# Local attention in two-step tiles beside RWKV's recurrence, with one PSUM bank for both chains

## The chip, the cores and the metric

One core of a Trainium2 chip runs the whole kernel. The metric is the device time of the program in microseconds; the median of three runs counts. A profiled execution of the same program gives the trace. Engines: PE is TensorE's matmul, PEld its weight load, DVE VectorE, ACT ScalarE, POOL GpSimd, SP SyncE, which here only issues DMAs.

## What is computed

Two layers over 512 latent and 256 context tokens, 1024 columns. Each layer: a modulated norm; one input projection whose columns go to four mixers (HGRN2, RWKV-7, windowed attention with sinks, multi-head latent attention); one output projection; a feed-forward block (dense in layer 0, eight experts in layer 1). Two of the mixers matter here.

```python
def rwkv7_scan(r, w, k, v, kk, b, s0, reverse):      # once forward, once backward
    def step(S, inp):
        r_t, w_t, k_t, v_t, kk_t, b_t = inp
        sa = jnp.einsum('bhvk,bhk->bhv', S, kk_t)
        S = S * w_t[:, :, None, :] - sa[..., None] * b_t[:, :, None, :] + v_t[..., None] * k_t[:, :, None, :]
        return S, jnp.einsum('bhvk,bhk->bhv', S, r_t)
...
def swa_mixer(p_lat, p_ctx, sink, cos, sin, ctx_out):
    ...
    mask = (jnp.abs(W + i - j) <= W)[None] & (s_abs >= 0) & (s_abs < T)
    s_loc = jnp.einsum('bkgnqd,bknsd->bkgnqs', qb, kw).astype(F32) * scale
    s_ctx = jnp.einsum('bkgnqd,bkcd->bkgnqc', qb, kc).astype(F32) * scale
    logits = jnp.concatenate([jnp.where(mask, s_loc, -jnp.inf), s_ctx, sink_l], axis=-1)
    prob = jax.nn.softmax(logits, axis=-1)
    o = (jnp.einsum('bkgnqs,bknsd->bkgnqd', prob[..., :3 * W], vw)
         + jnp.einsum('bkgnqc,bkcd->bkgnqd', prob[..., 3 * W:3 * W + Lc], vc))
    ...
```

Latent attention (`mla`) is softmax attention of four heads, in which a latent query sees all 768 keys and a context query the 256 context keys. In layer 1 (`last`) only latent tokens have an output.

## The kernel before

The program is written with a tile framework: the Python code issues instructions in an order, tiles of one name rotate through `bufs` buffers, and the framework sets the waits; the trace shows that it also moves an instruction that is ready ahead of one that is not. Generators are woven by `weave` (L243): each has a rate, and in every round the generators with rate 1 do one step, up to their next `yield`.

`mixers` (L1310) runs, per layer: projections with HGRN2's recurrence woven in (`columns`, L1415), then **the recurrence stage** (L1469 to 1480), then **the attention stage** (L1497 to 1529), then the rest of the output projection.

In the recurrence stage two directions (`rw_dir`, L648) each walk 12 chunks of 64 tokens in six pairs. For each pair a preparation (`rw_pair`, L718) loads decay W and key kk from DRAM (`s.rd`), forms the products BK and AR (r times W on POOL, L753), the matrices G, and an inverse by doubling: five levels of three steps. It has 19 steps; at most two preparations of a direction live at a time. Its matmuls go to four banks (`a00` to `a11`). A chain (`rw_chain`, L831) then does four steps a chunk: R, U, Z (the new state) and O (the output), each a group of matmuls into a bank of its direction (`c0` or `c1`, `psc`, L838) and an eviction; R and U are copied by VectorE and ScalarE, one half each (`pad`, L628). A third generator, `attention_prep` (L1449, rate 0.5), loads and prepares the queries and keys of both attentions in two banks named `hg` (`hps`, L347), and layer 0 computes two groups of modulation (`ada`, L414) through the same banks. Eight banks in all.

In the attention stage five generators are woven at rate 1: the read-outs of RWKV and HGRN2, `mla` (L1229), `swa` (L1164) and the loads of the first output weights. `swa` does, per block of 128 queries and per g, two tiles (kv = 0, 1): scores against two context key blocks and up to three neighbours, band additions in PSUM (L1186), `softmax` (L1107: sink copy, maximum, exponential with its sum, reciprocal, scaling, transposes into `pt`, copies into `PT`), then `heads_pv` (L1137: probabilities times values, two per key block and tile). Both attentions share three two-bank score buffers `sc`, one bank `pt` and one bank `pv`. `emit` (L1487) splits a result into two parts (a ScalarE cast and a POOL subtraction) for the output projection.

A matmul of float32 data is recorded as two instructions, a transpose as one.

## Time and profile before

| | us |
|---|---|
| median of 3 runs | 2664.5 (2660.79 to 2669.68) |
| profiled execution | 2658.14 |
| its span in the trace | 2656.0 |
| recurrence stage, layer 0 / layer 1 | 380 to 587 / 1669 to 1858 |
| attention stage, layer 0 / layer 1 | 587 to 731 / 1858 to 1958 |

A stretch is given in microseconds from the span's start. Busy times of an engine are the union of its instructions; PE's ends are modelled, and its matmuls overlap, so counts and distances between starts say more than its share. A line number can be that of a helper: L638 is `flip`, L328 `turn`, L633 `pad`, L276 the subtraction of a split.

### The profile page before, as it was taken

To read this page: it belongs to the slowest core of one execution; us is meant where nothing else is said; L and a number is where in the kernel's file an instruction comes from. 1 tells how busy PE (TensorE), PEld (TensorE's weight loads), DVE (VectorE), ACT (ScalarE), POOL (GpSimd) and SP (SyncE) were. 2 spreads that over 40 slices of the span, in tenths; PEclk is the share of its full clock that TensorE was granted. 3 is DMA by queue.
4 is the path that set the end of the run, shared out by engine and by line. 5 is a ranking of instruction groups with operands and counts; after the bars stand their busy time and mean duration, and the time that the engine had idled before them with its cause. 6 is when DMAs were issued, how large, how long until landed. Compare 5 with 4: busy or idle time off the path is not lost. (4 is left out here: it accounts for less than half of the span.)

```text
span 2656.0 us, 46639 instructions
## 1 busy us (share of the span) xinstructions
PE 2411.9 (91%) x18131; PEld 1991.5 (75%) x18131; DVE 1649.4 (62%) x3055; ACT 1240.9 (47%) x2348; POOL 487.5 (18%) x665
## 2 busy tenths in 40 slices
PE   7998779989998999999999998788996999999994
PEld 3887556666587888888877876566674898898993
DVE  5567946557568644344337597665745667667765
ACT  4744426556723211211237454565653556555653
POOL 1012345531011000000020222763202000000002
PEclk9999879999998999999999999799998899999997
DMA  6222142111053533334322323210213888887885
GB/s 225 84 82 93 65 139 69 32 39 56 1 165 125 153 117 115 120 114 128 112 71 67 97 73 120 72 30 8 72 36 101 271 266 274 277 268 259 264 273 175
DMA packets 190311, 339.28 MB, mean 128 GB/s; under 512 B 26465, under 2 KB 111201, under 8 KB 190081
## 3 DMA queue, kind: packets, MB, share of 16 engines
q1 hardware_dynamic: 183024, 310.39, 36.8%
q0 software_dynamic: 6480, 23.73, 2.5%
q8 instruction: 145, 2.38, 0.4%
q10 hardware_dynamic: 576, 2.10, 0.2%
q14 instruction: 86, 0.70, 0.1%
HBM read 305.88 MB, written 28.84 MB: 126 GB/s over the span
## 5 line engine op out<-in xcount | busy, mean ns | idle before, releaser
L288 PE MATMUL big<-hhi,hiw 128*128 128x512 f32 (+1 forms) x1504 | 523.7, 349 | 9.7 <-ACT hhi L510 3.8
L289 PE MATMUL big<-hlo,hiw 128*128 128x512 f32 (+1 forms) x1504 | 521.9, 347 | 1.7 <-DVE hlo L511 1.7
L290 PE MATMUL big<-hhi,low 128*128 128x512 f32 (+1 forms) x1504 | 519.7, 346 | 3.5 <-DVE low L276 2.3
L275 ACT CAST hiw<-raww 128x512 fp32r<-128x512 f32 (+3 forms) x208 | 158.3, 766 | 563.2 <-PE big L289 362.2
L288 PEld LDWEIGHTS big<-hhi,hiw 128*128 128x128 f32 x1504 | 286.3, 191 | 56.4 <-ACT hhi L510 8.1
L290 PEld LDWEIGHTS big<-hhi,low 128*128 128x128 f32 x1504 | 285.3, 190 | 44.4 <-DVE low L276 3.9
L289 PEld LDWEIGHTS big<-hlo,hiw 128*128 128x128 f32 x1504 | 285.9, 190 | 42.3 <-issue 4.0
L276 DVE TENSOR_TENSOR lom<-rawm,him 128x1024 fp32r<-128x1024 f32 x176 | 215.1, 1224 | 126.7 <-ACT him L275 125.1
L276 DVE TENSOR_TENSOR low<-raww,hiw 128x512 fp32r<-128x512 f32 (+3 forms) x202 | 184.7, 920 | 124.9 <-ACT hiw L275 123.3
L275 ACT CAST him<-rawm 128x1024 fp32r<-128x1024 f32 x176 | 184.3, 1047 | 148.8 <-PE sml L289 65.7
L288 PE MATMUL sml<-xh,him 128*128 128x256 f32 x528 | 151.9, 288 | 0.0
L289 PE MATMUL sml<-xl,him 128*128 128x256 f32 x528 | 149.4, 283 | 0.0
L290 PE MATMUL sml<-xh,lom 128*128 128x256 f32 x528 | 149.4, 283 | 0.0
L276 DVE TENSOR_TENSOR lov<-rawv,hiv 128x1024 fp32r<-128x1024 f32 x88 | 107.5, 1222 | 39.8 <-ACT hiv L275 39.6
L288 PE MATMUL sml<-him,xh 128*128 128x256 f32 x440 | 127.3, 289 | 0.6 <-DVE xl L276 0.6
L289 PE MATMUL sml<-lom,xh 128*128 128x256 f32 x440 | 125.3, 285 | 0.0
L290 PE MATMUL sml<-him,xl 128*128 128x256 f32 x440 | 125.1, 284 | 0.0
L289 PE MATMUL big<-gl,hiw 128*128 128x512 f32 (+1 forms) x352 | 119.5, 339 | 0.0
L288 PE MATMUL big<-gh,hiw 128*128 128x512 f32 (+1 forms) x352 | 118.9, 338 | 0.0
L290 PE MATMUL big<-gh,low 128*128 128x512 f32 (+1 forms) x352 | 118.2, 336 | 0.0
L275 ACT CAST hiv<-rawv 128x1024 fp32r<-128x1024 f32 x88 | 92.4, 1050 | 53.3 <-PE y L290 43.1
L455 DVE SCALAR_TENSOR_TENSOR raww<-raww,cb 128x1024 f32<-128x1024 f32 x56 | 68.6, 1225 | 69.1 <-DMA raww<-in_wadt 67.9
(551 smaller groups left out, 5618.3 us busy)
## 6 DMA issues: line engine op xcount, KB each, us to landing
rawm<-in_m SPq DMA_DIRECT2D x176, 512.0 KB, 5.1
rawv<-in_m SPq DMA_DIRECT2D x88, 512.0 KB, 4.9
raww<-in_wadt SPq DMA_DIRECT2D x56, 512.0 KB, 3.6
raww<-in_w SPq DMA_DIRECT2D x52, 512.0 KB, 3.9
raww<-in_winc SPq DMA_DIRECT2D x92, 256.0 KB, 2.9
raww<-in_wout SPq DMA_DIRECT2D x16, 512.0 KB, 3.7
wadt<-in_wadt SPq DMA_DIRECT2D x16, 512.0 KB, 4.2
raww<-in_w SPq DMA_DIRECT2D x16, 448.0 KB, 3.3
```

Source lines behind the costliest of these rows:

```text
L275: s.S.copy(hi, src)
L276: (eng or s.V).tensor_sub(lo, src, hi)
L288: s.E.matmul(out, ah, bh, start=start, stop=False)
L289: s.E.matmul(out, ah, bl, start=False, stop=False)
L290: s.E.matmul(out, al, bh, start=False, stop=stop)
L455: V.scalar_tensor_tensor(x, w, 1.0, cb[v], op0=OP.mult, op1=OP.mult, accum_out=m[:, v:v + 1])
```

## The change

Local attention moves from the attention stage into the recurrence stage: `attention_prep` goes on into `swa`, and its rate is 0.85 in layer 0 and 0.65 in layer 1. `softmax` is cut in three: maximum, exponential, and turn (reciprocal, scaling, transposes, copies). `swa` now has two steps a tile: the scores of a tile, then the turn of the tile before; then maximum and exponential of the new tile. The probabilities go to two fixed tiles (`turns`) in place of three rotating ones, and the exponentials to two buffers of 641 columns, which also serve as scratch for the ropes.

In PSUM, both chains take their R, U and Z from one bank `c`; O goes to the bank `pt`, which local attention uses for its transposes and its outputs; the two `hg` banks are replaced by one two-bank score buffer `sc`, of which `hps` takes the first half. Four `a` banks, `c`, `pt` and `sc` are eight. In SBUF, r leaves the pool that lives through the recurrence: its columns are written to DRAM behind the RWKV projection, and each preparation that needs r loads its part (`rq`). In the attention stage a generator `windows` splits local attention's results, 256 tokens a step, and `mla` keeps its buffers.

```diff
--- before.py
+++ after.py
@@ -346,6 +346,8 @@
 
     def hps(s):
 
+        if not s.nhg:
+            return s.ps("sc", 1024)[:, :512]
         return s.pp.tile([128, 512], F32, name="hg", bufs=s.nhg)
 
     def seg_gemm(s, lhsT, rhs, ntok, use, tag=None):
@@ -738,8 +740,10 @@
         P.tensor_copy(We, W[:, :, :, e:e + 1])
         AR = z['AR']
         BK = tp.tile([128, 2, 2, 2, 64], F32, name="BK" + nm)
-        kv, rv = tp.tile([128, 2, 2, 64], F32, name="kkq", bufs=2), v(g['r'])
+        kv, rv = (tp.tile([128, 2, 2, 64], F32, name=n, bufs=2) for n in ("kkq", "rq"))
         s.Q.dma_start(kv, v(s.rd[:, :2]))
+        if want:
+            s.Q.dma_start(rv, v(s.rd[:, 6:8]))
         bk = BK.rearrange("p c q t n -> p q t c n")
         V.tensor_mul(bk[:, 0], Wi, v(g['b']))
         P.tensor_mul(bk[:, 1], Wi, v(g['k']))
@@ -835,8 +839,8 @@
         AR, RP, UP = z['AR'], z['RP'], z['UP']
         c, vq, nm = ch - lo, z['v'], f"{d}"
 
-        def psc():
-            return s.ps("c" + nm)[:, :128].rearrange("p (t n) -> p t n", t=2)
+        def psc(tag="c"):
+            return s.ps(tag)[:, :128].rearrange("p (t n) -> p t n", t=2)
 
         def plus_state(out, a):
             for p in range(2):
@@ -861,7 +865,7 @@
             V.tensor_mul(Zn, Zn, We[:, :, c].to_broadcast([128, 2, 64]))
             yield
         if not (last and lo >= 8):
-            pO = psc()
+            pO = psc("pt")
             s.flip(pO, lambda p: G[:, c, 1, p, 1], lambda p: vq[:, c, p], True, False)
             s.flip(pO, lambda p: G[:, c, 0, p, 1], lambda p: UP[:, p], False, False)
             plus_state(pO, 1)
@@ -1104,9 +1108,9 @@
         for h, o in out or ():
             s.V.tensor_add(o[h, :LAT], x[h, :LAT], t[h])
 
-    def softmax(s, w, ps, scale, extra, tp, eng):
-
-        E, V, S = s.E, s.V, s.S
+    def softmax_max(s, w, ps, scale, extra, tp):
+
+        V = s.V
         n = w
         if extra is not None:
             V.tensor_copy(ps[:, w:w + 1], extra)
@@ -1117,15 +1121,21 @@
             V.tensor_scalar_mul(nm, nm, -scale)
         else:
             V.tensor_scalar(nm, nm, scale, -1.0, op0=OP.mult, op1=OP.mult)
-        pe = tp.tile([128, T], F32, name="pe", bufs=3)
+        return nm, n
+
+    def softmax_exp(s, ps, nm, n, scale, tp, pe):
         sm = tp.tile([128, 1], F32, name="sm", bufs=4)
-        S.activation(pe[:, :n], ps[:, :n], AF.Exp, bias=nm, scale=scale, accum_out=sm)
+        s.S.activation(pe[:, :n], ps[:, :n], AF.Exp, bias=nm, scale=scale, accum_out=sm)
+        return sm
+
+    def softmax_turn(s, w, pe, sm, p, eng):
+
+        E, V, S = s.E, s.V, s.S
         V.reciprocal(sm, sm)
         if eng is S:
             S.activation(pe[:, :w], pe[:, :w], AF.Copy, scale=sm)
         else:
             eng.tensor_scalar_mul(pe[:, :w], pe[:, :w], sm)
-        p = tp.tile([128, 6, 128], F32, name="PT", bufs=3)
         for a in range(0, w, 512):
             n = min(512, w - a)
             pt = s.ps("pt", 512, 1)
@@ -1134,8 +1144,15 @@
             (S.copy if a == 0 else V.tensor_copy)(p[:, a // 128:(a + n) // 128].rearrange("p a b -> p (a b)"), pt[:, :n])
         return p
 
-    def heads_pv(s, out, PT, nk, vts):
-        pv = s.ps("pv")[:, :128]
+    def softmax(s, w, ps, scale, extra, tp, eng):
+
+        nm, n = s.softmax_max(w, ps, scale, extra, tp)
+        pe = tp.tile([128, T], F32, name="pe", bufs=3)
+        sm = s.softmax_exp(ps, nm, n, scale, tp, pe)
+        return s.softmax_turn(w, pe, sm, tp.tile([128, 6, 128], F32, name="PT", bufs=3), eng)
+
+    def heads_pv(s, out, PT, nk, vts, tag="pv"):
+        pv = s.ps(tag)[:, :128]
         for j in range(nk):
             for i in range(2):
                 s.E.matmul(pv[64 * i:64 * i + 64], vts(i, j), PT[i][:, j], start=j == 0, stop=j == nk - 1)
@@ -1161,38 +1178,53 @@
                     S.copy(qp[g][hv[h], h, LAT:], q[hv[h], g, LAT:])
             yield
 
-    def swa(s, l, last, q, k, qp, vt, band, tp, emit):
-        E, V, S, P = s.E, s.V, s.S, s.P
-        nq = LAT if last else T
-        sk = s.sk
+    def swa(s, l, last, q, k, qp, vt, band, tp, turns):
+
+        E, V, S = s.E, s.V, s.S
+        sk, scale = s.sk, HD ** -0.5
+
+        def keys_of(blk):
+            return [4, 5] + ([n for n in (blk - 1, blk, blk + 1) if 0 <= n < 4] if blk < 4 else [])
+
+        def scores(blk, g, kv):
+            keys = keys_of(blk)
+            ps = s.ps("sc", 1024)
+            runs, at = [(512, 256)], 0
+            if blk < 4:
+                b0, nb = keys[2], len(keys) - 2
+                runs += [(128 * b0, 256)] + ([(128 * b0 + 256, 128)] if nb == 3 else [])
+            for ko, kn in runs:
+                E.matmul(ps[:, at:at + kn], qp[g][:, kv, 128 * blk:128 * blk + 128], k[:, ko:ko + kn], start=True, stop=True)
+                at += kn
+            for j, kb in enumerate(keys):
+                if j >= 2 and kb != blk:
+                    m = band[:, 0 if kb < blk else 1]
+                    V.tensor_add(ps[:, 128 * j:128 * j + 128], ps[:, 128 * j:128 * j + 128], m)
+            return ps
+
+        def turned(blk, g, kv, pe, sm):
+            keys = keys_of(blk)
+            PT.append(s.softmax_turn(128 * len(keys), pe, sm, turns[kv], (V, S)[kv]))
+            if kv:
+                s.heads_pv(q[:, g, 128 * blk:128 * blk + 128], PT, len(keys), lambda i, j: vt[:, keys[j], i], "pt")
+                PT.clear()
+        PT, ahead = [], None
         for blk in range(4 if last else 6):
             for g in range(2):
-                qs = slice(128 * blk, 128 * blk + 128)
-                keys = [4, 5] + ([n for n in (blk - 1, blk, blk + 1) if 0 <= n < 4] if blk < 4 else [])
-                w = 128 * len(keys)
-                PT = []
                 for kv in range(2):
-                    ps = s.ps("sc", 1024, 3)
-                    runs, at = [(512, 256)], 0
-                    if blk < 4:
-                        b0, nb = keys[2], len(keys) - 2
-                        runs += [(128 * b0, 256)] + ([(128 * b0 + 256, 128)] if nb == 3 else [])
-                    for ko, kn in runs:
-                        E.matmul(ps[:, at:at + kn], qp[g][:, kv, qs], k[:, ko:ko + kn], start=True, stop=True)
-                        at += kn
-                    for j, kb in enumerate(keys):
-                        if j >= 2 and kb != blk:
-                            m = band[:, 0 if kb < blk else 1]
-                            V.tensor_add(ps[:, 128 * j:128 * j + 128], ps[:, 128 * j:128 * j + 128], m)
+                    ps = scores(blk, g, kv)
+                    if ahead:
+                        turned(*ahead)
+                    yield
                     h = 2 * kv + g
-                    PT.append(s.softmax(w, ps, HD ** -0.5, sk[:, h:h + 1], tp, (V, S)[kv]))
-                s.heads_pv(q[:, g, qs], PT, len(keys), lambda i, j: vt[:, keys[j], i])
-                if blk % 2:
-                    c = slice(128 * blk - 128, 128 * blk + 128)
-                    emit(4 + g, c, q[:, g, c])
-                yield
+                    nm, n = s.softmax_max(128 * len(keys_of(blk)), ps, scale, sk[:, h:h + 1], tp)
+                    pe = tp.tile([128, 641], F32, name="pe", bufs=2)
+                    ahead = blk, g, kv, pe, s.softmax_exp(ps, nm, n, scale, tp, pe)
+                    yield
+        turned(*ahead)
+        yield
         for t in range(2):
-            s.tap(f"sw{l}{t}", q[:, t, :nq], slice(0, nq))
+            s.tap(f"sw{l}{t}", q[:, t, :LAT if last else T], slice(0, LAT if last else T))
 
 
     def mla_prep(s, l, last, cq, ckv, psf, scr):
@@ -1325,7 +1357,7 @@
             with ExitStack() as rx:
                 rp = rx.enter_context(s.pool("rec", side="right"))
                 g = {}
-                for n in ('r', 'k', 'b'):
+                for n in 'kb':
                     g[n] = rp.tile([128, 2, T], F32, name="rw" + n)
                 hgt, rwt = (x.rearrange("p a (c n) -> p (a c n)", n=64).rearrange(tok, c=12, t=2) for x in (hgo, rwo))
                 with ExitStack() as ax:
@@ -1336,7 +1368,7 @@
                     s.hhi = hh.tile([128, KT, T], F32R, name="hhi")
                     s.hlo = hh.tile([128, KT, T], F32R, name="hlo")
                     g['c0'] = s.wp.tile([128, 9], F32, name="rwc0")
-                    g['v'] = s.wp.tile([128, 2, T], F32, name="rwv")
+                    g['r'], g['v'] = (s.wp.tile([128, 2, T], F32, name=f"rw{n}") for n in 'rv')
                     g['yg'] = s.wp.tile([128, T], F32, name="rwyg")
                     g['tmp'] = lambda: s.wp.tile([128, T], F32, name="rwtmp", bufs=2)
                     g['yw'], g['ya'] = rwo[:, 0], rwo[:, 1]
@@ -1415,6 +1447,7 @@
                         def columns():
 
                             yield from s.rw_project(l, last, g)
+                            Q.dma_start(s.rd[:, 6:8, :nq], g['r'][:, :, :nq])
                             yield from s.rw_prep(l, last, g, s.wp)
                             if l == 0:
                                 s.clear_rows()
@@ -1437,7 +1470,7 @@
 
                     if l == 0:
                         yield s.ada(range(4, 6), lambda: tp.tile([128, 2, 512], F32, name="wada"),
-                                    s.hps, lambda: scr[0]), 6 / 64
+                                    s.hps, lambda: tp.tile([128, 2, 512], F32, name="wada")[:, 0]), 6 / 64
 
                 sq, cq, (ckv, sk) = hq, hk[0], (hz[0][:, i] for i in range(2))
                 f = it.rearrange("p a b c d -> p (a b c d)")
@@ -1466,18 +1499,20 @@
                     w = bp.tile([128, 512], F32, name="wk")
                     wk.append(w)
                     Q.dma_start(wk[0], s.I['wukv'][l])
+                    PT = f[:, 768:1408], tp.tile([128, 640], F32, name="PT1")
+                    yield from s.swa(l, last, sq, sk, qp, svt, band, tp, [x.rearrange("p (a b) -> p a b", a=5) for x in PT])
                 with s.pool("b") as tp, s.pool("pb", 1, PSUM) as s.pp:
                     done = set(), set()
-                    s.nhg = 2
+                    s.nhg = 0
                     wq, wk = bp.tile([128, 768], F32, name="wq"), []
-                    scr = [tp.tile([128, 512], F32, name=f"scr{i}") for i in range(2)]
+                    scr = [tp.tile([128, 641], F32, name="pe", bufs=2) for i in range(2)]
                     s.mskf = tp.tile([128, 2, 6, 64], F32, name="mskf")
                     mg = tp.tile([128, 512], F32, name="mg")
                     s.mg = mg.rearrange("p (d q n) -> p d q n", d=2, q=2)
                     Q.dma_start(mg, s.I['cst'][:, C_MG:C_MG + 512])
                     Q.dma_start(s.mskf, s.I['cst'][:, C_MSK:C_MSK + 768].rearrange("p (d h n) -> p d h n", d=2, h=6))
                     s.weave(*((s.rw_dir(d, last, g, rwt, *done, tp), 1) for d in range(2)),
-                            (attention_prep(s.hps), 0.5), *modulation(tp, scr))
+                            (attention_prep(s.hps), (0.85, 0.65)[l]), *modulation(tp, scr))
             with ExitStack() as ox:
                 hh = ox.enter_context(s.pool("oh"))
                 hhi = hh.tile([128, KT, T], F32R, name="hhi")
@@ -1514,10 +1549,15 @@
                         s.ow = ox.enter_context(s.pool("ow"))
                         for m in range(2):
                             load(m)
+                    def windows():
+                        for o in range(0, nq, 256):
+                            for k in range(2):
+                                emit(4 + k, slice(o, o + 256), sq[:, k, o:o + 256])
+                            yield
                     s.weave((s.rw_read(l, last, ld['v'], ld['yg'][:, 0], rwt, dp, emit), 1),
                             (s.hg_read(l, last, ld['gt'], hgt, dp, emit), 1),
                             (s.mla(l, last, cq, ckv, cstm, wq.rearrange("p (a b) -> p a b", a=2), wk[0], tp, dp, emit), 1),
-                            (s.swa(l, last, sq, sk, qp, svt, band, tp, emit), 1), (weights(), 1))
+                            (windows(), 1), (weights(), 1))
 
                     pss += [s.ps("sc", 1024, 3) for m in range(2)]
                     for o in range(0, nq, 256):
@@ -1973,7 +2013,7 @@
         s.yb = dp.tile([nrow, D], F32, name="yb")
         s.gd = dp.tile([128, 12, T], F32, name="gd")
         s.vd = dp.tile([128, 12, 128], F32, name="vd")
-        s.rd = dp.tile([128, 6, T], F32, name="rd")
+        s.rd = dp.tile([128, 8, T], F32, name="rd")
         s.setup()
         with ExitStack() as s.fx:
             s.mixers(0, False, s.I['xT'])
```

## Rows read from the trace of the kernel before

**Rows 1.** The page's first part: busy time, share of the span, instructions per engine.

```profile
PE 2411.9 (91%) x18131; PEld 1991.5 (75%) x18131; DVE 1649.4 (62%) x3055; ACT 1240.9 (47%) x2348; POOL 487.5 (18%) x665
```

**Rows 2.** Busy us per stretch: PE, PEld, DVE, ACT, POOL; clock, DMA share, GB/s.

```profile
380.00:390.00 10.00, 0.26 (x2) 0.26 (x4) 1.26 (x3) 4.30 (x8) 9.41 (x22) 0.50 0.82 213
390.00:587.00 197.00, 179.70 (x2365) 126.83 (x2364) 120.85 (x358) 107.03 (x344) 100.27 (x167) 0.98 0.15 42
587.00:638.00 51.00, 44.77 (x247) 30.39 (x246) 37.76 (x104) 28.68 (x64) 17.32 (x22) 0.97 0.18 57
638.00:731.00 93.00, 86.10 (x587) 55.84 (x587) 57.21 (x170) 69.36 (x161) 7.33 (x10) 1.00 0.09 32
1669.00:1690.00 21.00, 11.14 (x60) 7.96 (x60) 9.95 (x22) 8.92 (x16) 13.88 (x30) 0.50 0.44 119
1690.00:1858.00 168.00, 146.08 (x2128) 110.18 (x2129) 111.22 (x327) 98.43 (x327) 90.05 (x148) 0.99 0.08 20
1858.00:1902.00 44.00, 40.80 (x229) 26.42 (x227) 34.62 (x98) 27.69 (x60) 15.63 (x20) 1.00 0.27 84
1902.00:1958.00 56.00, 55.28 (x386) 37.72 (x384) 38.05 (x97) 42.78 (x88) 2.91 (x4) 1.00 0.06 20
```

**Rows 3.** Waits of the loader, 390 to 587: for whom, total us, times, longest.

```profile
PEld a L638 <- POOL AR L753: 8.8, 7, 1.9
PEld a L638 <- issue: 8.1, 35, 0.8
PEld a L638 <- ACT AP L633: 4.8, 15, 0.8
PEld a L328 <- DVE TU L817: 4.1, 12, 0.8
PEld c L638 <- issue: 3.7, 22, 0.2
```

**Rows 4.** Line L1181 alone, local attention's scores: PE, PEld busy in 1930 to 1958.

```profile
1930.00:1958.00 28.00, 0.00 (x0) 0.00 (x0) 1.00 0.00 1
```

**Rows 5.** Timeline, latent attention alone in layer 1: start us, duration, engine, instruction.

```profile
1940.88 1.52 PE L1141 MATMUL pv<-PT,mvt 128*64 128x128 f32 x22
...
1946.98 1.52 PE L1141 MATMUL pv<-PT,mvt 128*64 128x128 f32 x22
```

**Rows 6.** Waits of PE in layer 0's attention stage, 587 to 731: the largest.

```profile
PE pt L1133 <- ACT PT L1134: 4.3, 11, 0.9
```

**Rows 7.** Groups of 587 to 731 by form: busy us, mean ns; idle before, releaser.

```profile
L1141 PE MATMUL pv<-PT,it 128*64 128x128 f32 x176 | 17.2, 283 | 0.6 <-ACT mvt L1274 0.6
...
L1186 DVE TENSOR_TENSOR sc<-sc,it 128x128 f32<-128x128 f32 x24 | 7.0, 297 | 8.2 <-PE sc L1181 7.8
...
L1115 DVE TENSOR_REDUCE nm<-sc 128x1 f32<-128x641 f32 x8 | 6.6, 822 | 0.2
L1122 ACT ACTIVATE pe<-sc,nm 128x641 f32<-128x641 f32 x8 | 6.4, 796 | 4.6 <-DVE nm L1117 4.5
...
L1134 DVE COPY PT<-pt 128x128 f32<-128x128 f32 x8 | 2.3, 288 | 1.2 <-PE pt L1133 1.2
```

**Rows 8.** Timeline of the stage's end; last, from tile acc, the chains' U matmuls.

```profile
581.12 0.29 DVE L860 TENSOR_TENSOR Z<-c,Z 128x128 f32<-128x128 f32 x1
...
582.79 0.44 PE L638 MATMUL c<-v,G 128*64 128x128 f32 x4 [0.38 <-DVE xm L870]
...
583.92 0.26 ACT L633 COPY acc<-c 64x128 f32<-64x128 f32 x1 [2.50 <-DVE acc L633]
...
585.09 0.26 ACT L633 COPY UP<-c 64x128 f32<-64x128 f32 x1 [0.91 <-DVE UP L633]
...
L638 PE MATMUL c<-acc,TF x96: 270/273/324, 435.7 to 584.4; 128*64 128x128 f32 x96
```

**Rows 9.** Line L742, the kk loads: SP ns min, median, max; landing us.

```profile
L742 SPq DMA_DIRECT2D kkq<-rd x24: 359/365/468, 381.6 to 1788.2; - x24
...
DMA to landing us min/median/max: 2.0/2.2/2.3
```

**Rows 10.** Timeline: a 64-column weight load behind a 128-column transpose, in the recurrence.

```profile
508.67 0.19 PEld L638 LDWEIGHTS c<-acc,TF 128*64 128x64 f32 x2 [0.17 <-issue]
```

## Prediction

> **What bounds the kernel now.** I first read the page's engine totals [rows 1]: TensorE is marked busy 91% of the span, VectorE 62%, ScalarE 47%. That is an average over stages, so next comes the table by stretch [rows 2]. Each layer has a recurrence stage (380 to 587 in layer 0, 1669 to 1858 in layer 1) and behind it an attention stage (587 to 731 and 1858 to 1958) that ends where the output projection's first matmul starts. Only these four stretches, 640 us, are touched, apart from one store in the projections.
>
> The recurrence is not held by one engine. After its start, its weight loader (PEld) is busy 126.83 of 197 us in layer 0 and 110.18 of 168 in layer 1, so 70 and 58 us of it are idle; VectorE is at 61 and 66%, ScalarE at 54 and 59% [rows 2]. The loader's waits are many and short, at most 2 us each, on POOL, ScalarE and VectorE in turn [rows 3]: six small streams (per direction one chain and two preparations) step through all engines.
>
> The attention stage is different. Late in layer 1, when local attention has run out of score matmuls [rows 4] and latent attention runs alone, the order of TensorE repeats itself: from one group of 22 prob-times-value matmuls to the next pass 6.10 us [rows 5], nearly all of it filled. In that time two tiles of six key blocks of 128 are done, so **a key block costs 0.51 us** of a stage that TensorE sets. Its waits confirm it: of 144 us of layer 0's stage, the largest wait of TensorE is 4.3 us in total [rows 6].
>
> **What leaves the attention stage.** Local attention has 24 tiles in layer 0: eight of five key blocks, eight of four, eight of two, 88 blocks; layer 1 has 72 (eight of five, eight of four). The 176 prob-times-value matmuls of layer 0, two per block, agree [rows 7]. At 0.51 us, 88 and 72 blocks are 45 and 37 us, 82 together. The opening of that stage (latent projections, rope, its DMAs, read-outs: 51 us in layer 0, 44 in layer 1, with VectorE at 74 and 79% [rows 2]) had local attention as its filler. Without it some of its dependent steps show; I deduct 2 us per layer: **-78 us**. From below: if the opening kept half its length, 25 and 22 us, and 16 tiles of 3.05 us follow, layer 1 needs 71 us against 100 (-29), and layer 0, with eight small tiles more of two blocks (8 us), 82 against 144 (-62); that is 91 in all. From above, if the opening stays as long as it is, nothing of what ran inside it is won, and about 35 us remain. I keep 78, nearest to the measured period. The splits of the results (windows) stay in this stage beside latent attention: 0.
>
> **What it costs in the recurrence.** If nothing were hidden, 82 us come back; if all fits into the 70 and 58 us of idle loader time, 0. Which is nearer is read from VectorE, since it is the engine nearest to full there. Local attention's VectorE groups in layer 0 are twelve, from the band additions to the last small probability copy [rows 7]; with one division, one maximum, one negation and one sink copy per tile they sum to 43 us, in layer 1 to 33. VectorE would then have 120.85 + 43 = 164 us and 111.22 + 33 = 144 us of work [rows 2]. No stretch of these stages shows it above 79%; the 51 us opening, with as many streams, has 74%. At 74% the stages need 221 and 195 us, against 197 and 168: +24 and +27. At 79% they need 208 and 183: +11 and +15. ScalarE (107 + 44 us in 221, 68%) stays under the 75% that it shows in 638 to 731 [rows 2]. I take 74%: **+51 us**.
>
> **The shared bank.** Both chains now rotate through one bank for the three steps R, U and Z; O goes to the bank of the transposes. With nobody in the way, at the end of the stage, R holds its bank from 582.79 to 584.18 and U from 584.23 to 585.35 [rows 8]; Z, with eight matmuls like U's and one addition of 0.29 us in place of U's two copies, about 1.0 us (an estimate from those). Three uses take 3.5 us, 24 chunks 84 us, and the first U of the stage stands at 435.7 [rows 8], 151 us before its end. So the bank has 67 us to spare over 72 uses, and the chains mostly wait for the preparations anyway. TensorE, though, waits in order: behind a blocked R stand the preparations' matmuls. I count six chunks at the end, where no preparation is left, each with one ScalarE copy of 0.26 us more: 1.5 us per layer, **+3 us**; bounds 0 and, if each of 144 uses in both layers waits for one copy, +37.
>
> **Small parts.** The r columns take a detour through DRAM: one store in the projections, which TensorE bounds and 0, at most 4 (twice what the load below takes). Then 20 loads more on SP's queue, each right behind the kkq load, which lands in 2.2 us and costs SP 0.365 us [rows 9]; behind them on SP stand the second direction's loads, and POOL's product with r waits for them. That product is what TensorE's loader waits for longest in the recurrence, 8.8 us in layer 0 [rows 3], but it also stands behind ScalarE's exponential of W and POOL's own product before it, so the load has a cover: 0; where that is gone, 0.4 us a time over 20 times, 8 us. The preparation of attention runs at 0.85 and 0.65 steps a round in place of 0.5: it moves earlier inside the same stage, 0. Its matmuls, and layer 0's modulation with its four loads a group, borrow the one two-bank score buffer: local attention stands behind them. The 50 steps of layer 0 after some 14 preparing ones need 75 rounds at 0.85, about the rounds of the recurrence (19 steps a preparation, two at a time, three times, plus the start and the last chain); so a lag would show as a tail. I take 0, at most 27 us (eight tiles left over, each with nothing beside it at 3.4 us for maximum, exponential, scores and copies).
>
> **A rule weighed.** In the recurrence a 64-column block that follows a 128-column one shows a gap of 0.17 us marked "issue" [rows 10]; the loader's issue waits sum to some 12 us of layer 0 in its two largest rows [rows 3]. The Trainium skill, TensorEngine Tiling (Array Packing), section Tiling Modes, says that changing the tiling mode drains TensorE. The trace agrees in kind. It speaks against this change, since scores and transposes use the whole array and are now strewn among 64-column blocks. By rows: some three blocks a tile, two changes each at 0.17 us, 40 tiles: 41 us; in the attention stage about a quarter of them was paid already, so +30. As most issue gaps of today hide in waits for other engines, I don't add it; it is a rival.
>
> **Sum.** -78 + 51 + 3 = -24 us. The profiled execution took 2658.1 us, its span 2656.0; it lies 6.4 us under the median 2664.5 of the runs shown. So 2634 on its own scale, **2640** as a median.
>
> **The rivals.** *Hidden well:* VectorE reaches 79% or more and the opening shrinks as TensorE allows: -85 + 26 + 0 = -59, some 2605. For it speaks the idle loader; against it that each piece needs all three engines. *Width changes:* the 30 us are paid in full: -24 + 30 = +6, 2670, no change. A lag of eight tiles gives the same (+27). *Slower by longer steps:* the recurrence's length is a chain of steps, some 75 per layer, 146 in both. Each step evicts through VectorE and ScalarE, in order, and may find a softmax piece of 0.8 us (maximum 822 ns, exponential 796 ns [rows 7]) ahead of it. At 0.53 us more a step the 78 us are used up; at 0.68 us, 99 + 3 - 78 = +24: 2688. For it: the loader waits today on just such evictions; against it: with TensorE full of other work, part of a step's delay is overlapped by the other streams. That the bank alone decides it I hold for unlikely, as its 67 us of room must go first.
>
> **How the numbers follow.** Forecast 2640 (2625 to 2655) with 0.38, hidden well 0.25, width changes or a lag 0.15, longer steps 0.22. A measurement of this kernel can tell about 0.3%, 8 us, from no change. The forecast's upper end gives 0.02 to no change, the longer steps' lower end 0.01. So faster 0.61, same 0.17, slower 0.22. The range reaches from 2600 (0.05 lies below, where even more is hidden) to 2688 (half of the longer steps lies above): 2600 to 2688.
>
> **What would show it.** Right: latent attention's first score matmul some 20 to 30 us after the recurrence ends, then 3.05 us a tile; the attention stages near 100 and 66 us; the recurrence near 231 and 216 us with VectorE at 74%; no long wait on the c bank. Wrong: local attention's matmuls behind the last chain (a lag), issue gaps that double (widths), waits of loads for AP, TU and TT that grow from 0.3 to 0.6 us a time (longer steps), or waits of c matmuls on the other direction's copies (the bank).

## The result and the profile after

The median is 2683.45 us against 2663.08 us for the kernel before in the same runs: ratio 1.0069, 95% interval 1.0049 to 1.009. The change makes the kernel slower by some 20 us; 2640 was forecast. The profiled execution has a span of 2677.6 us, 21.6 more than before.

The engines' totals hardly moved against [rows 1]. First part of the page of the changed kernel:

```profile
PE 2421.7 (90%) x18131; PEld 1995.0 (75%) x18131; DVE 1643.8 (61%) x3055; ACT 1245.4 (47%) x2348; POOL 489.2 (18%) x665
```

From here on a **recurrence** reaches from the first product of AR with BK to latent attention's first q matmul, and an **attention stage** from there to the first matmul of the output projection. By stretch (busy us of PE, PEld, DVE, ACT, POOL; clock, DMA share, GB/s), first the two recurrences of the kernel before at these borders, then both stages of the changed kernel, in which the attention stage is cut at latent attention's first score matmul:

```profile
389.74:586.72 196.98, 179.68 (x2364) 126.81 (x2364) 120.85 (x358) 107.02 (x344) 100.51 (x167) 0.98 0.15 42
1679.49:1857.44 177.95, 153.87 (x2172) 115.16 (x2172) 118.58 (x339) 101.56 (x335) 96.60 (x159) 0.96 0.09 24
```

```profile
387.81:660.58 272.77, 239.24 (x2712) 168.38 (x2712) 157.92 (x494) 146.59 (x440) 100.69 (x167) 0.94 0.13 36
660.58:683.12 22.54, 20.36 (x71) 11.05 (x72) 14.96 (x30) 11.62 (x28) 19.54 (x26) 0.92 0.37 121
683.12:746.78 63.66, 59.87 (x401) 38.77 (x400) 41.92 (x105) 47.77 (x99) 4.81 (x7) 1.00 0.15 49
1697.08:1917.57 220.49, 196.74 (x2468) 146.09 (x2468) 143.39 (x443) 132.75 (x399) 98.43 (x159) 0.96 0.09 24
1917.57:1939.55 21.98, 16.81 (x54) 7.98 (x55) 13.52 (x26) 10.42 (x24) 16.73 (x22) 1.00 0.35 98
1939.55:1983.05 43.50, 42.16 (x263) 27.16 (x262) 29.21 (x64) 32.31 (x59) 1.45 (x2) 1.00 0.18 60
```

The attention stages gave back more than hoped: 86.2 and 65.5 us against 144 and 100 (587 to 731 and 1858 to 1958, [rows 2]), 93 us less. The recurrences took more than that: 272.8 and 220.5 us against 197.0 and 178.0, **118 us more**. VectorE, which was to be their limit at 74%, stands at 58 and 65%. PE is marked busy 88 and 89% of them.

One stretch of layer 0 shows at first sight why. Timeline of the changed kernel: two successive Z additions of the chains, between them the modulation's use of the score buffer sc, local attention's scores (L1197), and an O (bank pt) with the U behind it:

```profile
555.85 0.29 DVE L864 TENSOR_TENSOR Z<-c,Z 128x128 f32<-128x128 f32 x1
...
564.90 0.14 PEld L427 LDWEIGHTS sc<-wada,scp 128*32 128x32 f32 x4 [0.17 <-DMA wada<-in_wada]
...
567.80 1.32 PE L1197 MATMUL sc<-hz,hz 128*128 128x256 f32 x6
...
581.21 0.39 PE L640 MATMUL pt<-UP,G 128*64 128x128 f32 x4
...
582.43 0.27 DVE L635 COPY UP<-c 64x128 f32<-64x128 f32 x1
...
588.91 0.28 DVE L864 TENSOR_TENSOR Z<-c,Z 128x128 f32<-128x128 f32 x1
```

For 33 us no new state Z is made. The modulation holds the score buffer and waits for a DMA; local attention's scores come after it; O waits for pt, which local attention's turns use ahead of it; and the next U cannot be copied to UP, of which a direction has one, until O has read it. It looks like the cause, and it is what I tested first. It turned out to be a small part of it at most: layer 1 grew by 42 us with no such stall, its longest pause between two Z being 16 us (14 before).

### The profile page after: what moved, and what is told of

The parts are those of the page before. It is cut to its first block, busy times and chain, and to the rows that moved or that the text cites. A ratio compares the mean times of both kernels' runs of the same rounds, so it can differ in the third digit from the quotient of the medians.

```text
span 2677.6 us, 46644 instructions
## 1 busy us (share of the span) xinstructions
PE 2421.7 (90%) x18131; PEld 1995.0 (75%) x18131; DVE 1643.8 (61%) x3055; ACT 1245.4 (47%) x2348; POOL 489.2 (18%) x665
## 5 line engine op out<-in xcount | busy, mean ns | idle before, releaser
L276 DVE TENSOR_TENSOR lov<-rawv,hiv 128x1024 fp32r<-128x1024 f32 x88 | 107.5, 1222 | 33.7 <-ACT hiv L275 33.5
L797 POOL TENSOR_TENSOR Gm<-G,mskf 128x256 f32<-128x256 f32 x120 | 93.1, 785 | 149.3 <-PE a L640 146.9
```

Of the source, the lines that this page charges most:

```text
L276: (eng or s.V).tensor_sub(lo, src, hi)
L797: P.tensor_mul(x, G[:, :, 0, :, 0], s.mskf[:, 1 - d, i][:, None, None].to_broadcast(sh))
```

## The experiments

Theory 1: O queues in pt behind local attention. Theory 2: the bank c that both chains share. Theory 3: local attention's own instructions on the engines. Later expectations name finer forms: R is theory 1 again, P is theory 3 by TensorE's time, Q is theory 3 by softmax pieces that lie ahead of the chains' evictions on VectorE and ScalarE. The recurrence of the kernel before, in two later runs that leave it alone, took 198.0 us twice in layer 0 and 177.9 twice in layer 1, so a stage repeats within about 1 us.

**O back in c.**

```diff
-            pO = psc("pt")
+            pO = psc()
```

> The changed kernel with one edit: each chain's O goes back to the bank that its R, U and Z use (c), so that pt serves local attention alone. Theory 1 (my new one): O queues in pt behind the turns of local attention, whose tiles come late, and because each direction has one UP tile, which O reads, the next chunk's U cannot be written until O is done; the chains stand still. Then layer 0's recurrence falls from 281 us to 245 or less, layer 1's from 232 to 205 or less, and the time from 2683 to 2615-2640. Theory 2 (the one bank c for two chains is what costs): c gets a quarter more work, both recurrences grow, 2690 or more. Theory 3 (local attention's own instructions lie ahead of the chains' on the engines): 2675-2690, no stage moves by over 6 us.

Measured: 2700.3 us (ratio 1.0145, 1.0122 to 1.0168); windows of its recurrences:

```profile
389.31:662.11 272.80, 239.25 (x2712) 169.20 (x2712) 159.18 (x494) 146.53 (x440) 101.15 (x167) 0.92 0.13 36
1699.32:1933.00 233.68, 204.74 (x2469) 152.11 (x2469) 144.00 (x443) 133.00 (x399) 99.00 (x159) 0.91 0.09 23
```

The 33 us without a Z are gone (the longest pause in layer 0 is now 21 us), but layer 0's recurrence has the same length to 0.1 us and layer 1's is 13 us longer. The time is the one forecast for theory 2, but its growth shows in layer 1 alone. Theory 1 falls as the main cause. How much the stall was worth this run does not tell, since O in c has a price of its own: 13 us in layer 1, 8 of them as PE's busy time at a granted clock of 0.91 instead of 0.96. In layer 0 the price and what the stall had cost may have cancelled.

**The chains' bank plan alone**, in the kernel before.

```diff
-        def psc():
-            return s.ps("c" + nm)[:, :128]...
+        def psc(tag="c"):
+            return s.ps(tag)[:, :128]...
-            pO = psc()
+            pO = psc("pt")
```

> The kernel before with the bank plan of the chains alone: both directions take R, U and Z from one bank c, O goes to a bank pt of its own that nothing else uses; local attention stays in the attention stage and the two hg banks stay. Theory 1 and theory 3: the shared bank costs little; 2663-2675, recurrences 207-213 and 189-195 us. Theory 2: recurrences of 235 or more and 210 or more, 2700 or more.

Measured: 2676.5 us (1.0054, 1.0032 to 1.0076); the recurrences take 6.7 and 7.5 us more:

```profile
389.33:592.97 203.64, 183.13 (x2365) 128.09 (x2365) 117.52 (x358) 108.13 (x345) 101.55 (x167) 0.97 0.14 41
1689.35:1874.77 185.42, 157.47 (x2173) 117.98 (x2173) 114.83 (x339) 102.45 (x335) 97.65 (x159) 0.94 0.09 23
```

The shared bank costs 14 us by itself: real, but an eighth of the 118.

**The modulation moved to the attention stage** (there at rate 1, with three score buffers), alone and together with O in c.

```diff
-                            (attention_prep(s.hps), (0.85, 0.65)[l]), *modulation(tp, scr))
+                            (attention_prep(s.hps), (0.85, 0.65)[l]))
...
-                            (windows(), 1), (weights(), 1))
+                            (windows(), 1), (weights(), 1), *modulation(tp))
```

> The changed kernel with layer 0's two groups of modulation moved from the recurrence stage to the attention stage, where three score buffers stand; the one score buffer of the recurrence stage is then local attention's and its preparation's alone. Theory 1 with its cause in layer 0 (the modulation holds the score buffer from 398 to 440 and from 547 to 568 us, local attention is late by that, and O waits behind it): layer 0's recurrence falls by 30-50 us to 230-250, its attention stage grows by 5-15, layer 1 is unmoved, time 2640-2665. Theory 2 and theory 3: the recurrence falls by under 10 us, 2675-2690.

> Both edits at once: O back in the bank c and the modulation in the attention stage. Theory 1: what is left of the growth of the recurrences is the work of local attention and the shared c: layer 0 215-235, layer 1 195-205, time 2590-2630; the two edits overlap in layer 0, so their gains do not add there. Theory 2: 2685 or more. Theory 3: 2670-2690.

Measured: 2683.1 us and 2708.8 us. In the first, layer 0's recurrence is 246.0 us (26.8 less) and its attention stage 113.0 (26.8 more):

```profile
389.63:635.63 246.00, 221.07 (x2673) 163.59 (x2673) 155.84 (x486) 144.68 (x438) 100.46 (x167) 0.94 0.09 23
635.63:748.68 113.05, 98.97 (x511) 54.48 (x511) 57.72 (x142) 61.06 (x129) 23.93 (x32) 0.89 0.28 89
```

18 of the 26.8 us are the modulation's own PE work (239.24 to 221.07). It costs the same wherever it stands; that is the first hint. The other 8.6 us are pauses of PE that went with it, so theory 1's range for the stage held (230 to 250) and its time did not. The recurrences of the second run, in which O is in c as well:

```profile
388.35:647.17 258.82, 225.09 (x2673) 168.53 (x2673) 157.17 (x486) 145.44 (x438) 100.15 (x167) 0.91 0.08 22
1712.62:1945.44 232.82, 205.10 (x2468) 152.94 (x2468) 143.92 (x443) 133.17 (x399) 99.18 (x159) 0.90 0.09 23
```

Against the first run (246.0, and 219.3 in layer 1) O in c now costs 13 and 14 us. With the modulation in place it cost nothing in layer 0, so the stall was worth some 9 to 13 of layer 0's 76 us (an estimate from these runs).

**No bank shared with a chain.** Local attention's transposes and products go to its score buffer, first with O alone in pt, then with each chain wholly in its own bank.

```diff
-            pt = s.ps("pt", 512, 1)
+            pt = s.ps("pt", 512, 1) if room is None else room[:, a:a + 512]
...
-                    ps = scores(blk, g, kv)
                     if ahead:
                         turned(*ahead)
+                    ps = scores(blk, g, kv)
```

> The changed kernel; local attention's transposes and its probability-times-value products go to its own score buffer sc (a tile is turned before the next tile's scores), so that the bank pt holds nothing but the chains' O. Recurrences are counted from the first product of A, R with B, K to latent attention's first q matmul: before 197.0 and 178.0 us, after 272.8 and 220.5, with the chains' bank plan alone 203.6 and 185.4. Theory R (O and local attention hold each other up in pt): 235-250 and 195-205, time 2630-2655. Theory P (the stage is as long as TensorE's work at some nine tenths, and local attention brings 62 and 49 us of it): layer 0 at 250-273 (it may lose the stalls of the modulation), layer 1 at 215-222, time 2665-2690. Theory Q (softmax pieces lie ahead of the chains' evictions on VectorE and ScalarE): as theory P.

> As the run before it, and the chains go back to their own two banks, R, U, Z and O in the bank of the direction: no bank is shared between a chain and anything else. Theory R together with the shared c: recurrences of 215-235 and 185-195, time 2600-2630. Theories P and Q: 6 us a layer less than the run before it at most, 245-268 and 210-216, time 2650-2680.

Measured: 2715.7 and 2718.7 us, above every forecast. With everything in one score buffer local attention is late: in layer 0 its last scores start at 680.2 and 671.6 us, 36 and 42 us after the last Z. This spoils the totals, but the chains themselves can be read: from the first to the last Z of layer 1 they need 177 us in banks of their own, 167 in the changed kernel, 136 with the bank plan alone, 127 before. So in layer 1 sharing banks with local attention is not what slows them. In layer 0 the same four are 193, 216, 145 and 140 us. There the banks of their own come out shorter than the changed kernel, but a part of local attention's work lies behind the last Z, so these two runs do not settle it for layer 0.

**TensorE's part alone, and all but TensorE's part.** In the first run every score, transpose and product stays, on probabilities of zero, and the softmax is left out; in the second the softmax stays, on tiles in SBUF, and the matmuls are left out.

```diff
-            PT.append(s.softmax_turn(128 * len(keys), pe, sm, turns[kv], (V, S)[kv]))
+            for a in range(0, len(keys), 4):
+                pt = s.ps("pt", 512, 1)
+                for j in range(a, min(a + 4, len(keys))):
+                    E.transpose(pt[:, 128 * (j - a):128 * (j - a) + 128], turns[1][:, j], s.idn)
+            PT.append(turns[kv])
...
-                    nm, n = s.softmax_max(...)
-                    ahead = blk, g, kv, pe, s.softmax_exp(...)
+                    ahead = blk, g, kv, None, None
```

```diff
-            ps = s.ps("sc", 1024)
...
-                E.matmul(ps[:, at:at + kn], ...)
+            ps = stand
...
-                (S.copy if a == 0 else V.tensor_copy)(..., pt[:, :n])
+                (S.copy if a == 0 else V.tensor_copy)(..., pe[:, a:a + n])
-                s.heads_pv(...)
+                S.copy(q[:, g, 128 * blk:128 * blk + 128], p[:, 0])
```

> The changed kernel with TensorE's part of local attention alone: scores, transposes and products of every tile stay, on tiles of zeros; band additions, maximum, exponential, division, scaling and the probability copies are left out, so local attention's result is zero. Theory P: the recurrences stay at 245-273 and 210-220. Theory Q: 205-225 and 185-195, as without local attention. Theory R: shorter as well, 215-235 and 190-200, since the bank pt then comes free behind each transpose at once.

> The opposite: local attention's scores, transposes and products are left out, and its band additions, maxima, exponentials, divisions, scalings and copies run in the same order on tiles of the same size in SBUF (its result is no use). Theory P: recurrences of 205-225 and 185-192. Theory Q: 245-270 and 210-220. Theory R: 205-225 and 185-195, as pt is then O's alone.

**None, half and double.** Local attention left out; only its scores; TensorE's part issued twice.

```diff
-                    yield from s.swa(l, last, sq, sk, qp, svt, band, tp, ...)
```

```diff
-            for a in range(0, len(keys), 4):
-                pt = s.ps("pt", 512, 1)
...
-                s.heads_pv(...)
```

```diff
-            for ko, kn in runs:
+            for ko, kn in 2 * runs:
...
-            for a in range(0, len(keys), 4):
+            for a in 2 * list(range(0, len(keys), 4)):
...
-            if kv:
+            for _ in range(2 * kv):
                 s.heads_pv(...)
```

> The changed kernel with local attention left out altogether (its result is its rotated queries): what stays of the change in the recurrence is the bank plan, r through DRAM, the earlier preparation and the single score buffer. If these cost nothing beyond the shared bank (203.6 and 185.4 us with the bank plan alone): recurrences of 200-208 and 183-189 us. If r's detour or the single buffer cost what local attention's other engines seemed to cost (19 and 12 us without its TensorE part): 215-225 and 193-199.

> TensorE's part of local attention cut to its scores (29 and 24 us of its busy time in place of 62 and 49); transposes, products and all work of the other engines are left out, the result is no use. If TensorE's work adds to the stage in proportion (50 us for 62 and 33 us for 49 over the bank plan alone): 224-232 and 199-204. If the first half fits into idle time and the second does not: 204-212 and 185-190. If it is the 64-column blocks and transposes that cost, since each changes the width of the matmuls: the same low values.

> TensorE's part of local attention alone, as in the run without the other engines' work, and every score, transpose and product issued twice: some 124 and 98 us of TensorE work in place of 62 and 49. If the stage follows TensorE's work: 0.7 to 1.0 us for each added one, 295-315 and 251-267 us (253.3 and 218.1 with the single dose). If it was waiting and not work that made the stage long: under 275 and under 230.

Only the stages are compared for these: with TensorE's part alone, doubled, and without it, everything behind layer 1's attention stage takes some 75 us longer, presumably because the experts get other tokens from other values (2735, 2813 and 2688 us in all). Their recurrences, in the order none, scores, TensorE's part, double:

```profile
390.44:596.87 206.43, 182.77 (x2353) 127.45 (x2353) 119.32 (x354) 107.53 (x344) 102.46 (x167) 0.95 0.17 47
1631.89:1818.74 186.85, 157.52 (x2172) 117.61 (x2173) 115.42 (x339) 102.88 (x335) 99.13 (x159) 0.94 0.11 29
```

```profile
389.83:617.98 228.15, 206.77 (x2448) 143.18 (x2448) 120.78 (x354) 107.32 (x343) 102.81 (x168) 0.96 0.15 43
1661.70:1856.66 194.96, 172.82 (x2253) 127.95 (x2253) 118.09 (x339) 103.08 (x335) 99.10 (x160) 0.96 0.10 27
```

```profile
389.94:643.21 253.27, 228.06 (x2705) 161.92 (x2705) 121.65 (x354) 110.29 (x356) 101.46 (x168) 0.97 0.14 38
1680.03:1898.13 218.10, 197.55 (x2462) 148.62 (x2461) 114.88 (x339) 106.46 (x344) 98.00 (x160) 0.92 0.09 23
```

```profile
388.23:684.91 296.68, 273.18 (x3060) 196.93 (x3060) 125.79 (x354) 114.80 (x368) 102.26 (x168) 0.99 0.12 33
1730.32:1978.78 248.46, 227.93 (x2754) 172.49 (x2754) 118.19 (x339) 107.55 (x351) 99.14 (x160) 0.97 0.08 21
```

And without TensorE's part:

```profile
390.89:613.84 222.95, 183.83 (x2352) 127.58 (x2353) 154.35 (x489) 145.66 (x439) 101.78 (x167) 0.96 0.16 44
1652.05:1849.68 197.63, 164.29 (x2172) 118.78 (x2173) 142.10 (x438) 132.64 (x399) 98.86 (x159) 0.93 0.10 27
```

This settles the main question. TensorE's part alone brings 46.8 of layer 0's 66.3 us over "none" and 31.3 of layer 1's 33.6. PE's busy time grows by 45.3 and 40.0 us with it, so a microsecond of that costs 1.03 and 0.78. Doubled, TensorE's part brings 90.3 and 61.6: the second dose adds 45.1 and 30.4 us of PE time and costs 43.4 and 30.4, a price of 0.96 and 1.00, so there was no room left that the first had used up. In layer 0 the scores alone, 24.0 us of PE time more, bring 21.7. Only layer 1's scores came cheaper, 8.1 us for 15.3. The stage is its PE time and a remainder that stays (PE's ends are modelled, the lengths of the stages are not): length less PE busy is 24, 21, 25 and 24 us in layer 0 over the four doses, 29, 22, 21 and 21 in layer 1.

The other engines' work adds 16.5 and 10.8 us by itself; beside TensorE's part, in the changed kernel, it adds 19.5 and 2.4. Of the 19.5 us in layer 0, some 11 stand as more PE time for the same matmuls, at a granted clock of 0.94 instead of 0.97, and some 8 as a longer remainder (33.5 us); the stall of 33 us falls into this stage.

So theory 3, in the form of theory P, stands; without TensorE's part layer 1 lies above its 185 to 192, since the softmax is not free. The expectation for local attention's absence was right: what else the change brought costs 3 and 1 us over the bank plan alone. For the scores the proportional forecast held in layer 0 (228 in 224 to 232) and was too high in layer 1 (195.0 against 199 to 204); for the double dose it held at its lower end in layer 0 and missed by 2.5 us in layer 1.

**Smaller pieces.** Scores, turn, products, and maximum with exponential as steps of their own, woven in behind each direction.

```diff
+                    att = attention_prep(s.hps), (0.75, 0.57)[l]
+                    s.weave((s.rw_dir(0, last, g, rwt, *done, tp), 1), att,
+                            (s.rw_dir(1, last, g, rwt, *done, tp), 1), att, *modulation(tp, scr))
```

> The changed kernel with local attention cut into smaller steps (scores; turn; products; maximum with exponential), which are woven in twice a round, behind each direction, at a rate that keeps its pace; its work is the same. If TensorE's work as such sets the stage: recurrences within 6 us of 272.8 and 220.5, time 2675-2692. If it is the length of the pieces that stand ahead of the chains: 240-260 and 200-210, time 2635-2660, a version that beats both kernels.

Measured: 2689.6 us (1.0095, 1.0062 to 1.0128), recurrences 280.0 and 218.0, the first 1 us outside the 6 us allowed for TensorE's work, and far from 240 to 260. The length of the pieces is not it.

**The price where it stood before**, and a try at cutting it: local attention left out of the kernel before; and, in the kernel before, scores on the 64 rows that are not zero.

```diff
-                for kv in range(2):
...
-                    for ko, kn in runs:
-                        E.matmul(ps[:, at:at + kn], qp[g][:, kv, qs], k[:, ko:ko + kn], start=True, stop=True)
+                for ko, kn in runs:
+                    for kv in range(2):
+                        r = slice(64 * kv, 64 * kv + 64)
+                        E.matmul(two[kv][:, at:at + kn], qp[g][r, kv, qs], k[r, ko:ko + kn], start=True, stop=True)
```

> The kernel before with local attention left out (its result is its rotated queries): the price that it had in the attention stage. If it had the same price there as in the recurrence (98 us, from 2683 with it to 2586 without it), so that the move could not pay: 2565-2580, attention stages near 86 and 66 us. If the attention stage hid part of it: 2590-2610, attention stages of 100 or more and 75 or more.

> The kernel before with one edit: the score matmuls of a block's two tiles are issued in turn, each on the 64 rows that hold its own queries and keys (the other 64 rows of the padded queries are zero and were multiplied too), each into its own score buffer. Local attention stays in the attention stage. If TensorE's time is the currency of this stage and two matmuls on different rows run beside each other: scores cost half, 15 and 12 us of TensorE less, the attention stages 5-15 us shorter each, 2640-2655, a version that beats both kernels. If the two do not overlap, or the stage is set by the softmax pieces: 2655-2670.

The edit that leaves local attention out puts the splits of the changed kernel in its place:

```diff
-                            (s.swa(l, last, sq, sk, qp, svt, band, tp, emit), 1), (weights(), 1))
+                            (windows(), 1), (weights(), 1))
```

Without local attention the kernel before takes 2568.9 us and its attention stages 87.2 and 65.5 us, as forecast for the same price in both places. Local attention cost 57 and 35 us there, **92 together**; in the changed kernel it costs 66 and 34, **100 together**. By the times it is 94 (2663.1 less 2568.9) and 98 (2683.5 less 2585.6). The move hides nothing; it makes local attention slightly dearer, by 4 to 8 us.

The row pairs made the kernel slower: 2681.6 us (1.0077, 1.0064 to 1.0091), outside both ranges. Not for want of overlap: where the matmuls of the two tiles stand side by side, they start 6 to 14 ns apart and run beside each other. Layer 1's first group of eight instructions, and the same group in the kernel before:

```profile
1870.75 1.14 PE L1182 MATMUL sc<-hz,xm 64*128 64x256 f32 x8
```

```profile
1859.26 1.89 PE L1181 MATMUL sc<-hz,xm 128*128 128x256 f32 x8
```

But this holds for only 20 of the 88 pairs of instructions. Elsewhere a tile's matmuls run alone on their 64 rows, here after a wait for a score buffer, four in 1.13 us, no shorter than on all rows:

```profile
648.42 1.13 PE L1182 MATMUL sc<-hz,xm 64*128 64x256 f32 x4 [0.46 <-ACT pe L1122]
```

```profile
643.96 1.03 PE L1181 MATMUL sc<-hz,xm 128*128 128x256 f32 x4
```

All scores together are busy 48.3 us against 45.8. As both tiles of a block now take two of the three score buffers at once, latent attention's first matmuls wait for them, 5.3 us instead of 2.3; the way to its first scores grows from 50 to 57 us in layer 0 (43 to 54 in layer 1). Waits of PE in layer 0, 585.8 to 643:

```profile
PE sc L358 <- ACT pe L1122: 5.3, 2, 3.0
```

These waits are the smaller part of the growth. The attention stages of the row pairs, then those of the kernel before:

```profile
585.80:742.51 156.71, 143.78 (x830) 88.55 (x830) 94.77 (x274) 98.06 (x223) 24.37 (x32) 0.92 0.11 38
1868.84:1983.26 114.42, 107.42 (x612) 66.02 (x613) 71.46 (x194) 71.64 (x147) 18.59 (x24) 0.93 0.14 42
```

```profile
586.72:730.70 143.98, 130.85 (x830) 86.20 (x831) 94.96 (x274) 98.02 (x223) 24.65 (x32) 0.99 0.12 41
1857.44:1957.96 100.52, 96.60 (x613) 64.42 (x613) 72.76 (x194) 71.01 (x147) 18.54 (x24) 1.00 0.15 48
```

The stages grow by 12.7 and 13.9 us, and PE is busy 12.9 and 10.8 us longer for as many matmuls, at a granted clock of 0.92 and 0.93 instead of 0.99 and 1.00. Whether the waits or the half rows brought the clock down was not taken apart. So the run says nothing against row pairs that have their buffers free; that was not tried. No version here beats the kernel before.

## Why the prediction was wrong

| term | forecast, us | measured, us | from |
|---|---|---|---|
| attention stages | -78 | -93 | after less before |
| shared bank | +3 | +14 | bank plan alone |
| r through DRAM, earlier preparation, one score buffer | 0 | +4 | without local attention, less bank plan |
| local attention on TensorE | } +51 | +78 | TensorE's part, less none |
| local attention on the other engines | } | +22 | changed kernel, less TensorE's part |
| sum | -24 | +25 | spans: +21.6 |

The remaining 3.5 us lie outside these stages. Local attention's +100 is more than the 82 that the prediction gave for nothing hidden at all.

**Attention stages: right in kind.** Latent attention alone does two tiles in 6.10 us, as in [rows 5] (1972.07 to 1978.17 in layer 1), and its first scores come 22.5 and 22.0 us after the recurrence, in the 20 to 30 foretold. The deduction of 2 us a layer for the opening was wrong in sign for layer 0: the opening of 51 us [rows 2] became shorter, which is the working's "from below" (62 and 29, measured 57.8 and 35.0).

**The recurrence: the step that failed.** It is the sentence on the 70 and 58 us of idle loader time, "Which is nearer is read from VectorE, since it is the engine nearest to full there". The nearest to full stood in the same rows: PE, 179.70 of 197 and 146.08 of 168 us [rows 2], 17 and 22 us short of the stretch. I put it aside and took the weight loader as TensorE's room. VectorE's work came out as forecast (158 and 143 us against 164 and 144); its share did not, since it was not the limit. The loader's idle time was no room either: with the double dose it is busy 196.93 of 296.68 us, and each microsecond that the dose adds to PE still costs 0.96 and 1.00. The Trainium skill, Perfetto Trace Analysis, section Identifying the Most-Contended Engine, advises to judge TensorE's headroom by MFU (the share of peak arithmetic) and the busy share of the weight loads, and not by the busy share of the matmuls. On the weight loads this case's runs disagree: the loader stood at 64%, and next to nothing fitted in; MFU was not worked out.

The working already had the right yardstick. It priced a key block at 0.51 us of a stage that TensorE sets, 82 us in all, and took that out of the attention stage. The same 82 us put into the recurrence, with the 3 us of the bank, give -78 + 82 + 3 = +7 against the profiled execution; with the bank's measured 14, +18. Work was moved from one stretch that TensorE fills to another that it fills.

**The bank.** +14 instead of +3, within the bounds of 0 and 37. The count of room (67 us) was no argument: spread over the 144 uses it is 14.1/144 = 0.1 us a time, and it is paid although the room was never used up. How a use loses it was not taken apart.

**Small parts.** r's detour was rightly near 0: 4 us at most, as everything but the bank is in that row. No lag: the last scores start at 642.0 and 1898.5 us, 19 us before the stages end. The modulation was costed at nothing; it holds the score buffer and draws out a stall, but moving it won nothing, as it took 26.8 us more where it went.

**The rivals.** "Longer steps" had the right sign and nearly the right time, 2688, by a mechanism that the runs put at about a fifth: the softmax on VectorE and ScalarE brings 22 us of the 118, TensorE's work 78. Loader waits show it only in small: for TU they grew from 4.1 us, 12 times, to 5.2 us, 10 times (0.34 to 0.52 a time), for AP from 4.8, 15 times, to 4.9, 12 times (0.32 to 0.41), short of the 0.6 that was to show it and hardly more in all, against [rows 3]:

```profile
PEld a L640 <- issue: 13.4, 45, 0.9
PEld a L640 <- POOL AR L757: 12.5, 8, 2.2
PEld a L328 <- DVE TU L821: 5.2, 10, 1.7
PEld a L328 <- issue: 5.1, 11, 2.3
PEld a L640 <- ACT AP L635: 4.9, 12, 0.9
```

"Width changes" exist but are small. All issue waits of the loader together are 18.6 us before and 29.6 us after in layer 0, 14.2 and 17.8 in layer 1: 15 us, not all of it on the path, instead of 30. From none to TensorE's part alone they grow by 9.7 us while layer 0's recurrence grows by 46.8. The rule behind this rival was that of the Trainium skill, TensorEngine Tiling (Array Packing), section Tiling Modes, that a change of the tiling mode drains TensorE; the trace agrees in kind. The rival that was missing is the plain one: that the moved TensorE time is simply paid again.

The range of 2600 to 2688 holds the time; the direction, with 0.61 on faster, was wrong. (The parts named there add up to 0.18 for the same and 0.21 for slower, not 0.17 and 0.22.)

**What stays open.** Why the 21 to 29 us without PE in a recurrence cannot be filled was not taken apart; that they stay under every dose is shown. The largest row of PE's own waits in layer 0 is the wait for POOL's product AR, 11.5 us of the 25 with TensorE's part and 10.5 of the 24 with the double dose. What exactly the stall cost layer 0 is an estimate. Whether the chains could be kept from paying for the shared bank was not tried with local attention beside them in a way that did not make it late.

## What to carry to other kernels

Before work is moved into a stage that "waits a lot", charge it there at the same price at which it is credited where it leaves: if the same engine is nearly full in both, the move is worth zero, and only what it costs beside (a shared bank, a shared buffer) is left. Idle time of the weight loader, or many short waits, is no room; a cheap look is to leave the moved work out of both kernels and compare the two prices (92 and 100 us of the stages here). And a stall that is plain in the timeline is not yet the main cause: here the other layer grew without one, and the run that removed it left its stage as long as it was. An edit that removes a stall can bring a price of its own (13 us for O in c); read that price where there was no stall.

## What the hardware showed beside

- Float32 score matmuls of two tiles, on different halves of the rows and into different banks, ran beside each other where they stood side by side: eight instructions in 1.14 us against 1.89 us on all rows (1870.75 and 1859.26 above). Alone on 64 rows, four took 1.13 us against 1.03. The Trainium skill, TensorEngine Tiling (Array Packing), section Theoretical Speedup, gives up to a factor of two for a contraction of 64. This case's trace agrees in part, 1.66 in that group.
- In the stall of layer 0, PE is busy for only 2.60 of 5 us and its granted clock falls to the lower of its two levels, 1.2 GHz, for a time: a mean of 0.74 and 0.58 in two stretches of 5 us. So the matmuls that end a stall run slow as well: local attention's products take 0.42 us each at 577 us and 0.27 us at 590 us, where the clock is 1.00 again.

```profile
570.00:575.00 5.00, 2.60 (x8) 1.80 (x8) 2.29 (x6) 2.08 (x4) 0.00 (x0) 0.74 0.00 0
575.00:580.00 5.00, 4.34 (x34) 3.25 (x36) 1.05 (x5) 1.26 (x4) 0.00 (x0) 0.58 0.00 0
```
